# Conditioning and position-bias rows spread over 36 groups, and the first phase and the mixing listed anew by a planner that counts eight places for transfers

## The chip, the core and the metric

One core of a Trainium2 chip runs the whole kernel in one launch. The metric is device time in microseconds (us). The program keeps five queues going: TensorE (PE, with its weight loads PEld), VectorE (DVE), ScalarE (ACT), GpSimd (POOL, nearly unused here) and SyncE (SP), which issues every transfer (DMA). Each queue is worked off in its own fixed order; semaphores tie them together.

## What is computed

One residual block over 512 tokens of width 1024, one layer. Cut to what matters:

```python
mod = silu(c) @ w_ada + b_ada                       # 9 x 1024 numbers: shift, scale, gate of three sites
h = rmsnorm(x, g_ffn1) * (1 + sc1) + sh1
x = x + 0.5 * gt1 * swiglu(h, w_ffn1_in, w_ffn1_down)            # 1024 -> 2 x 2816 -> 1024
h = rmsnorm(x, g_mix) * (1 + sc2) + sh2
q_a, k_a, v_a, q_idx, k_idx, w_idx, c_q, c_kv, k_rope, gates = split(h @ w_in)
score = sum_h w_idx * relu(q_idx . k_idx)           # 8 index heads; the best 128 keys are kept
o_a = softmax(q_a . k_a / 8 + rel_bias[t5_bucket(pos_k - pos_q)], kept keys) @ v_a   # 8 heads, one k, one v
o_b = latent attention from c_q, c_kv, k_rope, causal by blocks of 64                # 8 heads
y = sigmoid(g_a) * (o_a @ w_o_a) + sigmoid(g_b) * (o_b @ w_o_b)
x = x + gt2 * (y @ w_out)
h = rmsnorm(x, g_ffn2) * (1 + sc3) + sh3
x = x + 0.5 * gt3 * swiglu(h, w_ffn2_in, w_ffn2_down)
out = rmsnorm(x, g_final)
```

Two side jobs feed this. **Conditioning** (`ada`): the product `silu(c) @ w_ada` is done as 72 reductions on DVE, each over one 512 KB block of `w_ada`; its result is one column of `mod`. **Position bias** (`t5_rows`): 32 blocks of rows of the bias are made with comparisons on DVE and ACT, 12 small matmuls, a copy on ACT and a transfer to memory; the sparse attention reads them back later.

## The kernel before

Activations lie with the channels on the 128 partitions and the 512 tokens along the free dimension. Every product is made of three float32r matmuls (high and low parts of weights and activations: `mm3`), each weight tile is split on ACT (`wh_...`, a cast) and DVE (`wl_...`, a subtraction).

The stages follow one another. First phase: inputs arrive, the first RMSNorm, and the first group of the first feed-forward layer (`first_group`, line 797: six PSUM banks of products that run through eight input blocks k; for each k the steps `w{k}` weights, `a{8+k}` and `a{k}` conditioning, `g{k}` gain, `m{k}..` modulated input, `f{k}..` products). Then the rest of the first feed-forward layer (`swiglu`, line 1018), the residual and norm at its end (`residual`, line 761: the last three output blocks are done in two halves of the tokens, the norm follows half by half), the mixing (line 1126: first group `hw`, `hm`, `hf`; then index scores `I`, top-k `T`, latents `L`, gates `G`, the two attentions `D`, `E`, `S`, `W`, the output projections `Y`, `O`), and the second feed-forward layer.

**Who sets the order.** While the program is built, `Plan.order` (line 473) plays the kernel through with a duration for each instruction. At each step it takes, on the engine that can start first, the instruction with the lowest place in a list among those that could start within `ahead` ns of the earliest; one that is on the list of urgent steps goes first if it could start within `share` of the other's cost. The order in which it starts them is the order of each engine's queue. Two stretches have lists of their own, `FIRST_ORDER` (line 48) and `MIX_ORDER` (line 87), with a cap for each kind of buffer (`FIRST_CAPS`, `MIX_CAPS`: how many of a kind may be held at once; `ix` are the PSUM banks of the index products, `ada` the blocks of `w_ada`). Elsewhere the program's own order holds. Buffers of one kind are handed out in the list's order of the instructions that fill them (`slot_time`, line 584). A transfer starts, in the plan, when the SP queue is free and its buffer is.

**The two side jobs in the first feed-forward layer.** `fill` (line 1644) is called 43 times, n = 1 to 43: after each of 19 pairs of hidden tiles and with each of 24 output tiles (eight in each of three groups of hidden tiles; the last eight are n = 36 to 43). Each call puts conditioning blocks into the program up to 56 n / `ADA_N`, and bias rows up to 10 + 22 n / `T5_N`:

```python
with nc.after(nc.last_pe):                      # the transfers wait for the matmuls so far
    while todo and 56 - len(todo) < max(min(2 * n, 8), 56 * n / ADA_N):
        self.ada(todo.pop(0))
...
while rows and 32 - len(rows) < T5_0 + (32 - T5_0) * n / T5_N:
    self.t5_rows(rows.pop(0))
```

A product's first matmul in a bank carries `start`, and every other one of that bank depends on it, so the products of k = 0 come first whatever the list says.

Of the kernel before, what the change touches and what calls it, by code (L numbers as in the profile page):

```python
# [19 lines left out]
I32 = mybir.dt.int32  # L20
# [25 lines left out]
URGENT = 2  # L46

FIRST_ORDER = """
t x10 g5 c d1 a0 x02 f10 f50 d5 m01 x03 m10 m00 w1 a11 x11 d4 m20 w0 x12 d0 a8 m11 a10 p n0 x13 f20 m21 g3 w2 m50
f40 f21 r6 f70 a9 g0 d6 r9 g2 a2 d2 m30 v r7 a1 n1 r2 r8 a3 x01 x00 a13 r5 f00 m40 f11 r3 a12 r4 g6 z f30 g4 a5  # L50
w6 m60 a4 r0 g7 w3 f60 r1 w4 m70 a6 d7 w5 w7 f01 a14 a15 d3 a7 g1
"""
FIRST_CAPS, FIRST_AHEAD, FIRST_SHARE = {"ada": 3, "adap": 128, "mt0": 41, "mt256": 110, "nrm": 90, "sg": 48, "t5m": 31, "t5o": 6, "whi": 68, "wlo": 59, "wst": 3}, 80.0, 0.10
FIRST_URGENT = """
c p x00 x01 v w2 n0 n1 f30 g7 m01 m40 f11 r9 f01 a7 a15 g1 m11 d0 m60 z g5 f50 a3 f00 d2 f40 m70 d7 g3 g0 w7 r7
f10
"""
# [25 lines left out]
"""  # L83

MIX_AT = 40
MIX_CAPS, MIX_AHEAD, MIX_SHARE = {"ava": 42, "avb": 20, "gate": 14, "gl": 2, "ix": 4, "lat": 14, "mg": 22, "mm": 60, "mt0": 1, "mt256": 27, "nrm": 32, "os": 7, "osa": 7, "yy": 3, "bias": 3, "mask": 7, "qa": 15, "wst": 1, "pA": 32, "pB": 18, "pTA": 25, "pTB": 36, "pe": 7, "rl": 46, "rn": 30, "score": 38, "t5": 16, "tpa": 24, "uhi": 26, "ust": 1, "wlo": 39, "y": 90}, 60.0, 0.30
MIX_ORDER = """
Yo0 B00 I30 hm00 B02 va Dx00 hf30 D01 hf60 S02 I36 hw1 hm01 hw0 hw5 hf10 S01 I31 u4 W00 L7 Lx4 hw2 Yg1 hf50 Wo1
L6 hm10 B10 W02 S03 I14 pq7 I21 qi1 i11 hw3 hw4 u0 B01 Yg4 I37 Yg3 S00 Ln4 I10 Wo2 L5 L4 hw6 W01 Wo0 Lx6 W12 S10
I35 A3 W10 Wo3 hm20 Yo6 hf20 hw7 L8 E000 i6 B11 I22 Uw I13 D00 ka B03 A1 S13 I26 pq5 pk6 S11 B13 I15 W11 pq2 kr  # L90
W20 W21 I17 I12 Wo5 i7 I16 A2 k1 Sn1 I11 T7 T13 B12 I20 I24 D10 G7 U2 W22 Yg2 pq4 U0 E101 B21 hf41 S12 G2 E201 R0
D02 G9 Lx5 pk2 B20 U3 Eo00 pk3 Yg0 W30 I23 i3 Lx7 i4 xs S23 hf31 i5 Pq0 pq3 S20 B22 k0 W31 i17 Eo10 G0 I32 pq0
Pk0 B31 hm70 E100 I34 B23 Pq1 I27 hm21 I33 hm50 Ln7 pq6 D03 S21 i2 G8 pk1 hf01 Dx10 U1 I25 i1 S22 Pk1 i0 W32 W40
R1 Pk2 i8 i15 hf61 W62 i16 W41 G1 pk5 Sn0 W50 G5 S30 W51 S33 S32 D11 hm41 hm60 T9 Yo1 i9 B30 S31 A0 S42 B32 Wo4
G4 S50 T6 hf71 Pq2 S41 D20 hz i18 W52 G6 B04 E202 u1 hf70 W42 qi3 S53 S40 Sn3 Yo2 G11 B16 T8 Yg7 hm30 E300 S51
qi2 qi0 D31 i10 hf21 ki D12 S52 i14 i12 S43 B33 T15 i20 D13 B14 W60 S60 Eo11 i13 u5 D23 D22 B07 i22 B17 i21 hf11
T10 i19 Wo6 E301 i24 Ya1 S62 Sn2 B06 G12 Yo5 E110 D30 k2 D21 B05 G3 Yb1 hm11 hm40 hm71 D32 i23 S61 D33 D04 S63
Lx8 Yb6 D07 Dx20 Ya0 Yb3 Yg5 Ya5 O2 D14 Ya7 B15 D17 E303 D06 Eo30 Yb0 B25 E302 Yb7 E200 D16 Ya6 D25 W61 Yo3 B37
E111 Ya4 B27 Yb2 hm61 E212 G13 Ya2 Wo7 B24 T12 hf40 T5 E210 hf51 Eo20 B35 O0 D37 Dx01 E312 D05 Sn7 W70 G10 Eo21
O4 Eo31 D27 D15 Sn6 Ya3 S72 O50 pq1 S70 O70 G15 k3 Yb5 Yb4 Yg6 E311 T4 O1 Dx11 Sn5 hf00 E313 B26 D26 u2 Ow5 W72  # L100
S71 hm31 O3 B34 T11 G14 O60 E010 Dx21 Yo4 O71 Pq3 On0 Dx30 E211 O61 D34 pk7 Dx31 D35 u3 D24 hm51 W71 Pk3 O51 pk0
E310 D36 T14 Ow7 Yo7 Sn4 Eo01 On1 pk4 B36 Ow6 S73
# [3 lines left out]
I34 I35 I36 u4 R0 k0 Pk0 pk0 pq1 i16 i11 S02 Sn0 W01 W02 S11 S12 pq2 pq3 W10 W12 Wo1 i18 Sn2 W21 B03 Dx00 Eo00
Sn3 i13 G6 W30 Wo3 Pk2 pq4 pk4 pq5 S40 S41 S42 D10 D11 D13 W42 Wo4 E100 T15 u3 Pq3 k3 Pk3 pk7 T11 D21 B22 S61 S62
S63 Sn6 W50 W51 W52 i12 D30 D31 D32 Dx30 D04 B05 D05 B06 G13 E201 Eo20 B14 D14 B16 D17 Dx11 D24 D25 Dx21 E302
E303 Eo30 E010 E111 i24 B34 D34 D35 B36 Dx31 E210 E211 E212 Eo21 S70 S71 S72 S73 E310 E312 E313 i19 W71 Yg0 Ya1
Yb1 Yb4 Ya5 Yb5 Ya6 On0 i0 G9 Dx01 B26 hf51 D01 I20 B27 hf01 I13 i21 D33 pk6 W62 B33 A1 D26 Ya4 Ow6 B13 hm01 hf61  # L110
# [231 lines left out]
class Plan:  # L342
# [130 lines left out]
    def order(self):  # L473
# [21 lines left out]
        self.free = {c: [(0.0, i) for i in range(n)] for c, n in SLOTS.items()}  # L495
        self.free[BANK] = [(0.0, i) for i in range(N_BANKS)]
        bw, clock, table, began, port = 0.0, Clock(), 1, 0.0, {"dve": 0.0, "pool": 0.0}
        for op in self.ops:
            if not op.left:
                ready[op.eng].append(op)  # L500
        done = []
        while len(done) < len(self.ops):
            best = None
            for e, lst in ready.items():
                if not lst:
                    continue
# [24 lines left out]
                best = (lo, r, op)
# [4 lines left out]
            _, s, op = best  # L536
            e = op.eng
# [6 lines left out]
            if e == "dma":  # L544
                x = max(s + op.hold + 625, bw)
                bw = x + op.cost
                op.end = bw
                free[e] = max(s + op.hold, bw - 3500)
            elif e == "pe":
                op.end = free[e] = s + op.cost * clock.factor(s)  # L550
                clock.busy(s, op.end, op.active)
                began = s
            else:
                op.end = free[e] = s + op.cost
                table = op.table or table
                if op.port:
                    port[e] = op.end
# [1138 lines left out]
```

## Time and profile before

| | us |
|---|---|
| median of three runs (1161.88, 1162.05, 1167.06) | 1162.05 |
| the profiled execution's own time | 1167.69 |
| its span, first to last instruction | 1165.7 |
| PE busy in the span | 1134.9 (97%) |
| DVE busy | 846.5 (73%) |
| ACT busy | 550.3 (47%) |
| mean granted TensorE clock, share of 2.4 GHz | 0.990 |

All durations below come from the profiled execution. In a row of a stretch, the number in brackets is the count of instructions, PEclk the granted clock as a share of 2.4 GHz (0.50 is 1.2 GHz), and the last two columns say how busy the transfer engines were and what they moved. In a row of the timeline the columns are start, length (of the merged instructions), engine, line, operation, output and inputs with their shapes; in brackets the engine's idle time just before it and what ended it. Every instruction of the plan has line 619, the call in `issue`, so one goes by the names of tiles.

### The profile page before, as it was taken

How to read it: one execution, taken by the hardware profiler on the slowest of the kernel's cores; microseconds unless marked ns; L12 is line 12 of the kernel's file. 1: busy time of each engine (PE TensorE's matmuls, PEld its weight loads, DVE VectorE, ACT ScalarE, POOL GpSimd, SP SyncE). 2: the span in 40 equal slices, each digit the busy share in tenths (PEclk: the TensorE clock that was granted, in tenths of full speed). 3: DMA queues.
4: the chain of work that ended last, by engine and by line, in shares of the span. 5: the costliest groups of instructions: out<-in, count | busy, mean ns of one | idle time of the engine just before them, and what ended most of it. 6: DMA issues, size and time to landing. Idle time of an engine off the chain costs nothing. (4 is left out here: it accounts for less than half of the span.)

```text
span 1165.7 us, 17532 instructions
## 1 busy us (share of the span) xinstructions
PE 1134.9 (97%) x6668; PEld 973.2 (83%) x6673; DVE 846.5 (73%) x1650; ACT 550.3 (47%) x1019; POOL 1.0 (0%) x7
## 2 busy tenths in 40 slices
PE   7999999999999999999999998999999999999996
PEld 5888888877887888887787776889999999999986
DVE  6975674558655785579999897757987877777746
ACT  5443333343333255545756678433564444445433
POOL 0000000000000000000000000000000000000000
PEclk9999999999999999999999999999999999999998
DMA  8645566557555743213233347431432333332122
GB/s 305 240 163 198 172 219 201 167 191 268 160 171 176 251 148 110 75 59 98 67 122 101 115 143 244 136 106 57 155 107 84 109 118 91 100 116 86 58 68 73
DMA packets 69590, 164.00 MB, mean 141 GB/s; under 512 B 10321, under 2 KB 22097, under 8 KB 69506
## 3 DMA queue, kind: packets, MB, share of 16 engines
q1 hardware_dynamic: 69506, 162.88, 43.5%
q8 instruction: 52, 0.85, 0.3%
q14 instruction: 32, 0.26, 0.1%
HBM read 148.11 MB, written 13.63 MB: 139 GB/s over the span
## 5 line engine op out<-in xcount | busy, mean ns | idle before, releaser
L619 DVE CUSTOM_DVE_ANT_0 junk<-ada,sc,vecs 128x1024 bf16<-128x1024 f32 x72 | 92.1, 1281 | 31.5 <-DMA ada<-in_w_ada_dram 31.4
L619 PE MATMUL bank<-hmh,wh_ib 128*128 128x512 f32 x200 | 80.5, 404 | 3.5 <-ACT wh_ib L619 2.5
L619 DVE SCALAR_TENSOR_TENSOR x<-bank,gt,x 128x512 f32<-128x512 f32 (+1 forms) x82 | 55.9, 682 | 34.2 <-PE bank L619 34.2
L619 PE MATMUL bank<-hml,wh_ib 128*128 128x512 f32 x200 | 80.5, 402 | 0.0
L619 PE MATMUL bank<-hmh,wl_ib 128*128 128x512 f32 x200 | 80.1, 401 | 0.1
L619 PE MATMUL bank<-hh,wh_1d 128*128 128x512 f32 (+1 forms) x197 | 74.0, 376 | 0.0
L619 PE MATMUL bank<-hl,wh_1d 128*128 128x512 f32 (+1 forms) x197 | 73.6, 374 | 0.0
L619 PE MATMUL bank<-hh,wl_1d 128*128 128x512 f32 (+1 forms) x197 | 73.6, 374 | 0.0
L619 PE MATMUL bank<-hl,wh_2d 128*128 128x512 f32 (+1 forms) x196 | 72.6, 371 | 0.0
L619 PE MATMUL bank<-hh,wh_2d 128*128 128x512 f32 (+1 forms) x196 | 72.4, 370 | 0.0
L619 PE MATMUL bank<-hh,wl_2d 128*128 128x512 f32 (+1 forms) x196 | 72.1, 368 | 0.0
L619 PE MATMUL bank<-f1h,wh_1g 128*128 128x512 f32 x152 | 59.5, 392 | 0.0
L619 PE MATMUL bank<-f1l,wh_1g 128*128 128x512 f32 x152 | 59.2, 389 | 0.0
L619 PE MATMUL bank<-f1h,wl_1g 128*128 128x512 f32 x152 | 59.2, 389 | 0.0
L619 PE MATMUL bank<-f1h,wh_1u 128*128 128x512 f32 x152 | 59.2, 389 | 0.0
L619 PE MATMUL bank<-f1l,wh_1u 128*128 128x512 f32 x152 | 59.2, 389 | 0.0
L619 PE MATMUL bank<-f1h,wl_1u 128*128 128x512 f32 x152 | 59.2, 389 | 0.0
L619 DVE TENSOR_TENSOR wl_1d<-ws_1d,wh_1d 128x896 fp32r<-128x896 f32 (+1 forms) x24 | 27.3, 1136 | 31.9 <-ACT wh_1d L619 21.2
L619 ACT CAST wh_1d<-ws_1d 128x896 fp32r<-128x896 f32 (+1 forms) x24 | 23.5, 979 | 54.5 <-DMA ws_1d<-in_w1d_dram 42.2
L619 PEld LDWEIGHTS bank<-hmh,wh_ib 128*128 128x128 f32 x200 | 38.1, 191 | 12.0 <-ACT wh_ib L619 2.8
L619 DVE TENSOR_TENSOR wl_1u<-ws_1u,wh_1u 128x1024 fp32r<-128x1024 f32 x19 | 23.2, 1223 | 33.5 <-ACT wh_1u L619 33.4
L619 PEld LDWEIGHTS bank<-hh,wh_1d 128*128 128x128 f32 x197 | 38.4, 195 | 7.9 <-issue 1.9
(2076 smaller groups left out, 3459.7 us busy)
## 6 DMA issues: line engine op xcount, KB each, us to landing
ada<-in_w_ada_dram SPq DMA_DIRECT2D x72, 512.0 KB, 4.5
ws_ib<-in_wib_dram SPq DMA_DIRECT2D x25, 512.0 KB, 3.6
ws_1g<-in_w1b_dram SPq DMA_DIRECT2D x19, 512.0 KB, 4.2
ws_1u<-in_w1b_dram SPq DMA_DIRECT2D x19, 512.0 KB, 3.7
ws_f<-in_w2b_dram SPq DMA_DIRECT2D x19, 512.0 KB, 3.7
ws_f<-in_w2b_dram SPq DMA_DIRECT2D x38, 256.0 KB, 3.6
ws_1d<-in_w1d_dram SPq DMA_DIRECT2D x16, 448.0 KB, 3.2
ws_2d<-in_w2d_dram SPq DMA_DIRECT2D x24, 256.0 KB, 2.7
```

The lines of the kernel that those rows point to most:

```text
L619: op.fn(*[real(v) for v in op.args], **{k: real(v) for k, v in op.kw.items()})
```

## The change

`T5_N` goes from 40 to 36 and `ADA_N` from 41 to 36. The lists, caps, `ahead`, `share` and urgent steps of the first phase and of the mixing are replaced. In `order`, a transfer may start no earlier than 1000 ns after the end of the eighth-last transfer; that rule holds in all stages, while the orders of the two feed-forward layers after the first group are not listed.

```diff
 FIRST_ORDER = """
-t x10 g5 c d1 a0 x02 f10 f50 d5 m01 x03 m10 m00 w1 a11 x11 d4 m20 w0 x12 d0 a8 m11 a10 p n0 x13 f20 m21 g3 w2 m50
-f40 f21 r6 f70 a9 g0 d6 r9 g2 a2 d2 m30 v r7 a1 n1 r2 r8 a3 x01 x00 a13 r5 f00 m40 f11 r3 a12 r4 g6 z f30 g4 a5
-w6 m60 a4 r0 g7 w3 f60 r1 w4 m70 a6 d7 w5 w7 f01 a14 a15 d3 a7 g1
+d5 a1 t n0 p d7 x10 d0 m00 x01 f20 x03 m01 v f10 g3 w2 g0 d6 m10 d1 g2 m20 f30 f60 a8 x02 a9 r3 n1 a11 g1 g7 m11
+d2 r8 a0 g6 w0 g5 d3 a2 x11 f50 g4 c f01 x12 m21 w1 m30 w3 f21 a7 x13 r6 z m40 f70 a10 x00 f11 r5 r1 r0 f40 r4 a3
+m50 m60 w4 a12 a13 a4 w5 a5 w6 r2 a14 d4 r9 r7 a15 m70 a6 w7 f00
 """
-FIRST_CAPS, FIRST_AHEAD, FIRST_SHARE = {"ada": 3, "adap": 128, "mt0": 41, "mt256": 110, "nrm": 90, "sg": 48, "t5m": 31, "t5o": 6, "whi": 68, "wlo": 59, "wst": 3}, 80.0, 0.10
+FIRST_CAPS, FIRST_AHEAD, FIRST_SHARE = {"ada": 23, "adap": 146, "mt0": 58, "mt256": 145, "nrm": 117, "sg": 63, "t5m": 38, "t5o": 13, "whi": 78, "wlo": 73, "wst": 2}, 60.0, 0.00
 FIRST_URGENT = """
-c p x00 x01 v w2 n0 n1 f30 g7 m01 m40 f11 r9 f01 a7 a15 g1 m11 d0 m60 z g5 f50 a3 f00 d2 f40 m70 d7 g3 g0 w7 r7
-f10
+c p x00 x01 v n1 x03 w2 x02 r6 m60 x11 r7 x12 a6 a1 m50 m01 m30 m11 g4 a12 a15 x13 f10 d4 r3 r5 a11 d1 w7 d2 g2
+g0 f11 a4 w6 r2 a0 a2 m00 f50 g1
 """
-T5_0, T5_N, ADA_N = 10, 40, 41
+T5_0, T5_N, ADA_N = 10, 36, 36
...
-MIX_CAPS, MIX_AHEAD, MIX_SHARE = {"ava": 42, "avb": 20, "gate": 14, "gl": 2, "ix": 4, "lat": 14, "mg": 22, "mm": 60, "mt0": 1, "mt256": 27, "nrm": 32, "os": 7, "osa": 7, "yy": 3, "bias": 3, "mask": 7, "qa": 15, "wst": 1, "pA": 32, "pB": 18, "pTA": 25, "pTB": 36, "pe": 7, "rl": 46, "rn": 30, "score": 38, "t5": 16, "tpa": 24, "uhi": 26, "ust": 1, "wlo": 39, "y": 90}, 60.0, 0.30
+MIX_CAPS, MIX_AHEAD, MIX_SHARE = {"ava": 31, "avb": 20, "gate": 15, "gl": 3, "ix": 1, "lat": 4, "mg": 15, "mm": 49, "mt0": 7, "mt256": 26, "nrm": 33, "os": 2, "osa": 13, "yy": 5, "bias": 3, "mask": 3, "qa": 19, "wst": 1, "pA": 33, "pB": 17, "pTA": 32, "pTB": 31, "pe": 10, "rl": 53, "rn": 17, "score": 22, "t5": 15, "tpa": 19, "uhi": 20, "ust": 1, "wlo": 38, "y": 67}, 20.0, 0.30
 MIX_ORDER = """
...
 MIX_URGENT = """
...
+        self.lanes = [0.0] * 8
...
-                    r = max(op.ready, t + 1500.0 * (op.table not in (0, table)), began + op.load if e == "pe" else 0.0)
+                    r = max(op.ready, self.lanes[-8] + 1000.0 if e == "dma" else 0.0, t + 1500.0 * (op.table not in (0, table)), began + op.load if e == "pe" else 0.0)
...
                 bw = x + op.cost
                 op.end = bw
+
+                self.lanes.append(bw)
```

`MIX_ORDER` and `MIX_URGENT` are whole new lists of the same steps (some 560 in the order).

## Rows read from the trace of the kernel before

**Rows 1.** Busy time by stretch, whole kernel but the tail.

```profile
0.00:30.00 30.00, 22.27 (x214) 16.05 (x217) 20.41 (x82) 17.27 (x47) 0.70 (x6) 0.94 0.90 307
30.00:68.00 38.00, 37.85 (x227) 32.02 (x228) 36.44 (x77) 19.18 (x34) 0.00 (x0) 0.96 0.65 230
60.00:403.00 343.00, 343.00 (x1729) 280.45 (x1728) 211.04 (x306) 120.00 (x171) 0.31 (x1) 1.00 0.61 197
403.00:428.00 25.00, 21.26 (x140) 19.84 (x139) 20.89 (x62) 11.24 (x22) 0.00 (x0) 0.86 0.39 126
428.00:525.00 97.00, 96.07 (x532) 82.28 (x530) 61.44 (x105) 51.64 (x86) 0.00 (x0) 1.00 0.28 91
525.00:650.00 125.00, 121.28 (x578) 95.72 (x577) 121.36 (x321) 78.79 (x183) 0.00 (x0) 0.99 0.29 92
650.00:735.00 85.00, 80.03 (x422) 62.64 (x424) 69.57 (x194) 65.59 (x161) 0.00 (x0) 1.00 0.55 179
735.00:1150.00 415.00, 415.00 (x2832) 385.38 (x2831) 302.75 (x493) 189.94 (x322) 0.00 (x0) 1.00 0.31 96
```

**Rows 2.** Busy time by stretch: the three places where the clock falls.

```profile
29.00:34.00 5.00, 5.00 (x33) 4.28 (x33) 4.61 (x13) 1.36 (x4) 0.00 (x0) 0.57 0.99 357
405.00:413.00 8.00, 7.79 (x40) 7.77 (x40) 4.59 (x19) 2.19 (x5) 0.00 (x0) 0.57 0.41 126
526.00:532.00 6.00, 4.11 (x11) 3.26 (x12) 5.82 (x11) 3.93 (x7) 0.00 (x0) 0.72 0.28 92
```

**Rows 3.** Timeline of DVE at the end of the first feed-forward layer.

```profile
399.26 0.42 DVE L619 TENSOR_TENSOR acc_n<-acc_n,sq_n 128x256 f32<-128x256 f32 x1
401.92 1.28 DVE L619 CUSTOM_DVE_ANT_0 junk<-ada,sc,vecs 128x1024 bf16<-128x1024 f32 x1 [2.24 <-DMA ada<-in_w_ada_dram]
403.13 0.48 DVE L619 SCALAR_TENSOR_TENSOR x<-bank,gt,x 128x256 f32<-128x256 f32 x1
403.53 1.28 DVE L619 CUSTOM_DVE_ANT_0 junk<-ada,sc,vecs 128x1024 bf16<-128x1024 f32 x1
404.73 0.42 DVE L619 TENSOR_TENSOR acc_n<-acc_n,sq_n 128x256 f32<-128x256 f32 x1
```

**Rows 4.** Timeline of PE there.

```profile
402.90 0.28 PE L619 MATMUL bank<-hh,wl_1d 128*128 128x256 f32 x1
403.02 0.28 PE L619 MATMUL bank<-hh,wh_1d 128*128 128x256 f32 x1
405.20 0.87 PE L619 MATMUL bank<-ones,acc_n 128*128 128x2 f32 x4 [1.91 <-DVE acc_n L619]
406.93 0.41 PE L619 MATMUL bank<-hh,wh_1d 128*128 128x256 f32 x1
407.14 0.41 PE L619 MATMUL bank<-hl,wh_1d 128*128 128x256 f32 x1
```

**Rows 5.** Timeline of SP: the last two conditioning blocks are issued.

```profile
395.25 0.86 SPq L619 DMA_DIRECT2D ada<-in_w_ada_dram  x2
```

**Rows 6.** Busy time by stretch: output tiles of the first group of hidden tiles.

```profile
125.00:175.00 50.00, 50.00 (x302) 40.52 (x301) 33.99 (x54) 18.47 (x31) 0.31 (x1) 1.00 0.63 203
```

**Rows 7.** Timeline of the first phase: ACT, DVE and PE.

```profile
4.82 1.06 ACT L619 ACTIVATE sc<-c 128x1024 f32<-128x1024 f32 x1 [2.40 <-DMA c<-in_c_dram]
11.98 4.98 PE L619 MATMUL bank<-x 128*128 128x128 f32 x24 [1.36 <-DMA x<-in_xT_dram]
24.31 4.97 PE L619 MATMUL bank<-ones,sq_n 128*128 128x2 f32 x32
27.10 1.27 DVE L619 SCALAR_TENSOR_TENSOR mf1h<-x,a,bank 128x256 f32<-128x256 f32 x3
29.81 0.58 PE L619 MATMUL bank<-f1h,wh_f 128*128 128x256 f32 x1
```

**Rows 8.** Timeline of PE in the mixing.

```profile
527.89 0.50 PE L619 MATMUL bank<-hmh,wh_ib 128*128 128x512 f32 x1 [2.03 <-ACT wh_ib L619]
```

**Rows 9.** What SP waited for from 505 to 530 us: total, times, longest.

```profile
SPq L619 <- DVE wl_uk L619: 9.7, 1, 9.7
SPq L619 <- ACT gl L619: 8.2, 1, 8.2
```

**Rows 10.** The tile `rl`, ACT's reading of the index products: ns, first and last start.

```profile
L619 ACT ACTIVATE rl<-bank x24: 380/492/606, 468.2 to 526.1; 128x512 f32<-128x512 f32 x8, 128x256 f32<-128x256 f32 x8, 128x384 f32<-128x384 f32 x8
```

More of the change, by code (lines that the diff above doesn't have):

```diff
@@ L87 @@
 MIX_ORDER = """
[L88 to L102, printed above, removed]
+hf31 hf70 u0 S00 hw0 hm30 hw4 Wo0 Yg6 S01 S02 u4 S03 hw1 I10 Lx6 Dx00 I14 qi0 I31 pq7 pq6 I30 pk6 hm00 hw2 W00
@@ new lines @@
+B00 I13 B02 Yg4 B11 D01 E100 I21 pq5 S10 hw5 L7 Yo6 I37 B01 Yg1 hm20 i1 W02 Uw hf41 Lx4 hw3 I22 i17 I36 D02 L6 L5
+I16 L4 A3 W01 E000 I12 u1 B03 k0 Wo1 W12 B10 hm10 qi1 i7 D00 S13 hw7 W10 S11 hw6 va W11 hf20 hm21 Lx5 A1 kr I15
+I26 W21 i20 ka L8 A2 I17 I11 I20 B21 U1 B13 W22 S12 Ln4 Yo4 E101 G7 G2 Wo3 U0 I24 Sn1 W20 I35 pk3 W30 pq2 B12 T15
+R0 Lx7 G9 U2 i6 D10 I23 pq0 Pq0 S23 pq3 U3 B20 i0 i9 i5 B22 i4 I32 W31 I25 Dx10 hm50 D20 Pk0 S20 I27 B31 i3 S21
+pk5 hf71 i8 Ln7 hm01 Yg5 Pq1 E201 W32 Pk1 pk1 I33 W40 i2 D03 B23 B30 S22 Eo00 hf00 I34 G0 G8 B32 pk4 Yg2 k1 R1 G5
@@ new lines @@
+pk2 W62 G1 S32 W50 S30 S33 hm61 S31 T10 W41 T8 B04 S42 B14 D11 S50 E202 hf21 W51 B33 Yo1 i16 Sn3 hm71 u5 B16 i11
+Pk2 S41 G4 D31 A0 Lx8 W42 O70 E301 i18 S40 S51 i10 W52 Pq2 i14 Sn2 S52 T7 S43 Yo0 S53 i13 T13 i15 i12 D12 S60 G6
+Yg0 i19 Wo4 D13 G3 hf51 B07 G12 ki i22 Sn4 i21 S61 i24 S73 T5 D23 E110 Yg3 E200 Ya1 D30 D22 Yo3 xs Sn0 B17 G11
+E300 D21 Wo5 T4 D32 Yb1 Wo6 Eo10 Wo7 Pq3 hf30 D33 k2 Yo5 i23 S63 B05 D04 Yb6 hm41 qi3 D07 B06 pq4 Yb7 W61 D14 T9
+Ya5 E303 Wo2 E302 D17 hf11 E212 D06 O50 G13 Eo20 W60 hm31 B25 hf60 Ya0 qi2 S62 Dx20 D25 B37 pq1 Ya4 pk7 G10 Eo11
@@ L103 @@
+T12 Yb5 Ow7 B15 Ya2 O1 hf50 Eo30 D37 T6 Ya7 Yb3 Eo01 Yb0 E111 Yo2 Eo21 D05 D15 Dx11 Ya3 W70 D16 O2 E210 Ya6 S72
+D27 E211 Dx21 E311 B24 G15 D26 Yb4 hm11 S70 Pk3 Ow6 hf61 hz W71 k3 Yb2 Ow5 hf10 Dx01 O3 T11 u2 hm60 S71 Eo31 D24
+Dx31 O0 Yg7 B27 B34 T14 hf40 O60 Sn7 O4 E010 B26 E313 O51 hf01 Yo7 Sn5 D35 O71 hm40 On0 E310 O61 B36 E312 D34
+hm70 Dx30 pk0 hm51 D36 G14 On1 W72 u3 Sn6 B35
 """
 MIX_URGENT = """
-hz hm00 hm11 hf11 hm20 hm21 hf50 hf60 xs qi1 qi3 kr i1 I10 I15 I16 I17 Ln4 i7 L7 Lx7 Lx8 I22 I23 I24 I25 I26 I32
@@ L106 @@
[L106 to L110, printed above, removed]
@@ L111 @@
-hf71 I12 hm70 hf41 pq7 B23 B00 i2 qi0 Eo10 i3 B07 hm10 hf21 i15 Uw D22 W11 pk3 hw7 D15 D06 L5 B31 D02 Ow5 i4 hm30
-Ow7 B11 D23 hf20 hf31 Yo7 B02 E301 hw2
+hm11 hm30 hm31 hm40 ki qi0 I15 I16 Ln4 Lx7 Lx8 I22 I23 I24 I26 I35 R0 k0 pk0 i11 Sn0 S11 S12 pq2 pk2 pq3 W10 Wo1
+i18 Sn2 B00 Dx00 Sn3 i13 G6 W30 Pk2 pk4 pq5 S40 S41 B11 D11 Wo4 E100 u3 Pq3 k3 Pk3 pk7 D21 S61 S62 S63 Wo5 i12
+D31 i22 G13 E201 Eo20 D16 Dx11 B25 Dx21 E303 Eo30 E010 E111 D34 D35 Dx31 E210 E211 E212 S70 S71 S73 E310 E311
+E312 E313 i19 W71 Yo0 Yb4 Ya6 O1 On0 Dx01 I12 S51 hm51 Eo00 Lx5 pk6 Yo4 i2 I21 Ya2 E101 D25 E110 W01 E301 pk5 I31
@@ L113 @@
+D20 B20 B27 B30 T7 D07 B23 i14 hm01 hm71 O4 S23 hf30 D12 Ow5 W00 D06 Eo21 B15 Yo1 D14 B35 hf21 D17 Yo5 B06 i16
+hw7 W41 qi2 U0 D02 hm70 D10 W11 L5 Yo2 hf51 O70 Yg2 E202 A1 i7 S33 hw3 hf50 hf01 D22 i15 hf70 hw2 Ow6 pq7 hf10
+E200 B21 S31 S00 W20 u0 i8 i5 I34 W72 Yg6 xs Yg3 D24 hf60 Yg4 D30 hm10 Yb0 B04 i9 S72 D05 Wo6 W52 D04 u1 hm20 Sn5
+hf71 I30 D37
 """
```

## The prediction

> **What bounds the kernel now.** I read the busy time by stretch first. From 60 to 403 us and from 735 to 1150 us PE has no idle time at all and the full clock [rows 1]: there the end is set by the matmuls alone, the change takes none away and adds none, and no order of other queues can make these 758 us shorter. What can change lies in three places. In the first 30 us PE is busy for 22.27, so 7.7 us are idle; from 30 to 68 us it is busy for 37.85 of 38, while DVE is busy for 36.44, so DVE keeps up only just [rows 1]. From 403 to 428 us, where the first feed-forward layer hands over to the mixing, 3.7 us of PE are idle. In the mixing 0.9 us are idle up to 525, 3.7 from 525 to 650 and 5.0 from 650 to 735; in the middle one of these DVE is busy for 121.36 of 125 us, so it is DVE that paces it, and in the stretch before, DVE still has 35.6 us free [rows 1].
>
> The second view is the granted clock. Three spells are at 1.2 GHz instead of 2.4. A mean of 0.57 over 5 us is 5 x 0.43 / 0.5 = 4.3 us at half speed, which costs 2.1 us; 0.57 over 8 us is 6.9 us, a cost of 3.4; 0.72 over 6 us is 3.4 us, a cost of 1.7 [rows 2]. The second and the third follow an idle PE: 1.91 us before 405.20 and 2.03 before 527.89 [rows 4, 8].
>
> Last, the timelines around these places say who was late.
>
> **How the execution stands to the median.** The profiled execution took 1167.69 us (span 1165.7, so 2.0 around it), the runs 1161.88, 1162.05 and 1167.06. The median is 5.6 us below the execution in which I read my rows. The spells of slow clock cost 7.2 us together in that execution, and I cannot see whether the shorter runs have them all. I therefore count idle time in full and the cost of a slow spell by half when I go down from the median, and in full when I go down from 1167.69.
>
> **The conditioning and the bias rows.** Before, the 56 conditioning blocks were complete only at n = 41, the first half of the third-last output tile. SP issues the last two at 395.25 [rows 5], and DVE, which works in order, sits idle for 2.24 us until one lands at 401.92, reduces it in 1.28 us, does one residual add at 403.13, reduces the other from 403.53 and only then adds the squares for the norm at 404.73 [rows 3]. PE is at its last matmul at 403.02, and waits 1.91 us for exactly that sum [rows 4]. Behind the two reductions on DVE stand the residual add, the sum of squares and so the norm, and behind the norm the whole mixing; ACT's squares wait for the residual add.
>
> With 36 both jobs are complete at n = 36, the first of the last eight output tiles, four full tiles and a half earlier. A full tile is 7 blocks of 3 matmuls of 512 columns; at two half tiles of 0.12 us a matmul [rows 4] that is 21 x 0.24 = 5.0 us, so the last block is asked for about 22 us earlier, near 373. Without the two reductions the sum of squares would be there 2 x 1.28 = 2.56 us earlier even if nothing is credited for the wait for the transfer: at 405.15 - 2.56 = 402.6, before PE asks at 403.3. So the stall of 1.91 us goes, and with it very likely the slow spell behind it: matmuls of 256 columns follow each other every 0.21 us there instead of 0.12 [rows 4]. Next late is the norm's own chain, which PE has to cover with the two half tiles that are left, 42 x 0.12 = 5.0 us; I allow 0.5 us for that. This is worth 1.91 + 3.4 - 0.5 = 4.8 us in the profiled execution and 1.91 + 1.7 - 0.5 = **3.1 us** from the median; the bounds are 0 (another late step on DVE takes their place) and 5.3.
>
> The work itself is moved, not removed. Per call it becomes 56/36 - 56/41 = 0.19 more blocks, 0.24 us of DVE and 0.1 MB, and 0.06 more bias rows. Beside output tiles of 5 us DVE has 16 of 50 us free and the transfer engines are busy at 0.63 [rows 6]; over the whole stretch DVE is busy for 211 of 343 us [rows 1]. I cost this at nothing. Without that cover it would be 0.24 us a call, 8.6 us over 36 calls. SP issues the same transfers, five or six calls earlier, and past them the first weights of the mixing move up.
>
> **The first phase.** PE begins the feed-forward products at 29.81 [rows 7]. Ahead of them in its queue stand 4.97 us of squares sums from 24.31, and DVE makes the first modulated input only at 27.10. How early can they begin with the new lists? Buffers are handed out in list order, so the conditioning blocks come as 1, 8, 9, 11, 0; k = 0 needs blocks 8 and 0, and its products must be first. Before block 0 has landed, some 5.8 MB must have: x with 2.1, c with 0.5, five blocks with 2.6, one tile of weights and the constants with 0.6. At the 307 GB/s of the first 30 us [rows 1] that is 18.9 us, so about 20 us; a reduction of 1.28, one modulation of 0.4 and the cast bring 23 to 24, an estimate. The gain at the start is thus at most 5.8 us. On the other side c, the first transfer before, now comes behind a block, the constants and a weight tile, some 1.1 MB or 3.6 us: `silu(c)`, begun at 4.82 [rows 7], begins near 8.4, and every conditioning reduction waits for it. If DVE loses that much it is a loss of 3.6 us, since DVE paces the 38 us that follow. Between a gain of 5.8 and a loss of 3.6 I take **2.5 us of gain**: nearer to the gain, as the 24 products of x that the norm needs end at 17 [rows 7], and the 12 us from there to the first product are queueing on DVE and PE more than data that had not come; but less than half of it, because DVE has to do the same work in the stretch up to 68.
>
> **The mixing's list and the eight places.** The one large stall is that before 527.89: 2.03 us of PE and the 1.7 us of slow clock behind it, for a weight tile that came late [rows 2, 8]. SP's waits just before were for a DVE subtraction (9.7 us) and an ACT copy (8.2 us), not for an earlier transfer [rows 9], so the rule of eight places doesn't remove it by itself; a list that places these steps anew may or may not. The bounds: all idle time from 428 to 735 and this spell, 9.6 + 1.7 = 11.3 us of gain; a loss of 11.8 us (the second rival). I take half of the one stall, (2.03 + 0.85) / 2 = **1.4 us of gain** (1.9 in the profiled execution), as DVE, at 97% from 525 to 650, leaves an order little room [rows 1]. In the second feed-forward layer the rule only moves transfers in SP's queue; PE has no idle time there, and I cost it at nothing; if a weight tile came late there, one such stall is the 3.7 us of 527.89.
>
> **Sum.** From the median: 1162.05 - 3.1 - 2.5 - 1.4 = **1155.0**. A profiled execution like that before: 1167.69 - 4.8 - 2.5 - 1.9 = 1158.5.
>
> **The rivals.**
>
> 1. The lists bring nothing and only the handover gains: 1162.05 - 3.1 = 1159. For it speaks that DVE paces both listed stretches and its work stays; against it, that PE waits in both for order and not for DVE's throughput alone [rows 7, 8]. A like time, 1158, comes out if the change doesn't do what it says, the last blocks still landing late because SP's queue holds them back, while the lists gain their 3.9.
>
> 2. Slower: the index products lose their banks. The cap `ix` falls from four PSUM banks to one. There are 24 such products, and ACT reads each in 0.492 us [rows 10]. If PE must wait for each reading before the next product, that is 24 x 0.492 = 11.8 us, 1155.0 + 11.8 = 1166.8, and one more fall of the clock of the 2.6 us between the two in the mixing and the handover [rows 2] makes it 1169.4. It decides from 0.29 us a product (7.0 / 24), where the gain is eaten. Against it: PE has the large products of the input projection to put between, and up to 525 it is idle for 0.9 us only [rows 1]. The Trainium skill, Perfetto Trace Analysis, section Matmuls, speaks for this rival: independent groups of matmuls should rotate through PSUM banks, so that the reading of one overlaps the next. No run here shows one bank; by that rule the time would be that of this rival, by the row of 0.9 us idle the forecast's.
>
> 3. Everything is gained: 5.8 in the first phase, the full 4.8 at the handover, half of the 11.3 in the mixing: 1162.05 - 16.2 = 1146. It needs DVE to run ahead before 525.
>
> **How the numbers follow.** The forecast holds 0.50 of the chance (1152 to 1158.5, three fifths of it below 1156.2), the first rival with its variant 0.20, the second 0.11, the third 0.19. About 0.5%, 5.8 us, is what a measurement of this kernel can tell from no change. Faster by more than that (below 1156.2): 0.30 + 0.19 = 0.49; within: 0.20 + 0.20 = 0.40; slower: 0.11. The range goes from 1147 to 1167; it leaves out the slow rival and the lower half of the third.
>
> **What would show it.** Right: no conditioning reduction on DVE after about 385 us, no PE wait for `acc_n` at the end of the first feed-forward layer and full clock there; the first feed-forward product before 27 us and the first one after the first group before 67; no PE wait over 1 us for `wh_ib`. Wrong: a new wait of PE in place of that for `acc_n`, a feed-forward start later than 30 us with DVE waiting for `sc`, PE waiting for `rl` again and again between 460 and 530, or PE idle time after 735.

## The result and the profile after

The changed kernel takes 1154.44 us (median; 1153.21 to 1155.74), the kernel before beside it 1162.05 us; the ratio is 0.9924 with a 95% interval from 0.9902 to 0.9945. The forecast was 1155.0. Its sum came out near by luck: two of its three terms have the wrong size and nearly make up for each other, as the experiments show.

Busy time by stretch of the changed kernel, in the columns of [rows 1]; the stages now end up to 13 us earlier, so the later stretches begin a little further on in the work:

```profile
0.00:30.00 30.00, 23.41 (x225) 16.80 (x226) 21.48 (x85) 17.51 (x49) 0.70 (x6) 0.91 0.95 313
30.00:68.00 38.00, 38.00 (x232) 32.67 (x232) 36.30 (x71) 18.49 (x29) 0.00 (x0) 0.98 0.64 226
60.00:403.00 343.00, 340.98 (x1701) 277.10 (x1701) 214.27 (x316) 122.50 (x178) 0.31 (x1) 1.00 0.61 196
403.00:428.00 25.00, 23.67 (x191) 22.95 (x190) 22.57 (x65) 12.83 (x25) 0.00 (x0) 1.00 0.47 142
428.00:525.00 97.00, 94.51 (x501) 80.02 (x500) 68.97 (x140) 48.39 (x80) 0.00 (x0) 0.98 0.30 93
525.00:650.00 125.00, 124.00 (x616) 98.78 (x616) 118.58 (x308) 85.85 (x201) 0.00 (x0) 1.00 0.30 97
650.00:735.00 85.00, 84.80 (x439) 68.78 (x438) 69.95 (x173) 61.38 (x148) 0.00 (x0) 1.00 0.57 188
```

From 525 to 735 us PE's idle time falls from 8.7 us [rows 1] to 1.2. From 403 to 428 us PE does 2.4 us more, at full clock. From 428 to 525 us DVE does 69.0 us of work where it did 61.4 [rows 1]. And there are 2.0 us of idle time in the first feed-forward layer, which had none. Waits of PE over the whole changed kernel (in all, times, longest, us):

```profile
PE bank L622 <- DVE dg_n L622: 4.3, 3, 2.5
PE bank L622 <- DVE posf L622: 2.5, 1, 2.5
PE bank L622 <- ACT t5m L622: 1.8, 1, 1.8
...
PE bank L622 <- ACT kil L622: 1.1, 1, 1.1
PE bank L622 <- ACT wh_ib L622: 0.7, 1, 0.7
```

The waits for `acc_n` [rows 4] and the 2.03 us for `wh_ib` [rows 8] are gone. The 1.8 us for `t5m`, a mask of the bias rows, stand at 257 us and are new there; the kernel before waits 0.8 us for one, at 21 us.

The stages of all runs, by the starts of products in PE's timeline: the first product after the first group, the last one of the first feed-forward layer, the first one of the second. "Mixing" is from the second to the third; the second feed-forward layer takes 350.1 to 350.3 us in the four profiles of the two kernels.

| kernel | first group ends | layer 1 | mixing |
|---|---|---|---|
| before | 68.1 | 346.1 | 389.6 |
| before, again | 69.4 | 341.6 | 389.5 |
| changed | 65.1 | 345.1 | 380.2 |
| changed, again | 66.5 | 342.8 | 378.9 |
| `ADA_N` 41 | 66.4 | 344.2 | 382.2 |
| both numbers back | 67.3 | 341.5 | 382.8 |
| no rule of eight | 67.2 | 343.2 | 380.8 |
| old first list | 67.0 | 341.2 | 380.0 |
| old mixing list | 66.5 | 342.6 | 388.2 |
| top-k late | 66.4 | 343.4 | 388.6 |
| DVE work at 530 to 580 | 66.5 | 343.0 | 385.0 |
| DVE work at 448 to 456 | 66.6 | 342.0 | 388.6 |
| DVE work at 514 to 530 | 66.0 | 342.4 | 388.1 |
| weights first | 66.8 | 376.3 | 380.6 |

The kernels below ran in three groups, each on a chip of its own beside the kernel before, so they are compared by their ratio to it. For the changed kernel that is 0.9924 and, run again, 0.9909; I use 0.9917. A thousandth is 1.16 us, and each ratio is uncertain by 1.2 to 2.6 thousandths either way.

### The profile page after: what moved, and what is told of

Same layout as the page of the kernel before. It is cut to its first block, busy times and chain, and to the rows that moved or that the text cites. A ratio compares the mean times of both kernels' runs of the same rounds, so it can differ in the third digit from the quotient of the medians.

```text
span 1152.7 us, 17526 instructions
## 1 busy us (share of the span) xinstructions
PE 1129.1 (98%) x6673; PEld 969.7 (84%) x6673; DVE 847.2 (73%) x1650; ACT 548.0 (48%) x1019; POOL 1.0 (0%) x7
## 4 chain that ended last, share of the span: by engine, by line
PE 90%; DVE 6%; DMA 2%; ACT 1%; issue 1%; SPq 0%; DVEq 0%; ACTq 0%
PE bank L622 90%; DVE score L622 1%; DMA ws_1d<-in_w1d_dram 1%; DMA x<-in_xT_dram 1%; DVE tiny_top L622 1%; DVE tiny_norm L622 1%; DVE tiny_mla L622 0%; DMA ws_ib<-in_wib_dram 0%; DVE mhmh L622 0%; DVE junk L622 0%; DVE qa L622 0%; DVE wl_ib L622 0%; DVE o L622 0%; DVE hml L622 0%; ACT qa L622 0%
```

## One part undone at a time

**The numbers of 36.**

```diff
-T5_0, T5_N, ADA_N = 10, 36, 36
+T5_0, T5_N, ADA_N = 10, 36, 41
```

> The changed kernel with ADA_N back at 41, so that the last conditioning blocks come at n = 41 again; T5_N stays at 36. Theory (the handover gains by the earlier blocks): DVE reduces two blocks after 395 us again, PE waits 1 to 2 us for acc_n at the end of the first feed-forward layer, with slow clock behind it, and the time is 1154.4 + 3.1 = 1157.5 (up to 1159.2 with all of the slow spell). If the new stall at 257 us (1.8 us idle and about 1.7 us of slow clock) comes from the denser conditioning blocks, it is gone here and gives 3.5 back: 1154 to 1156, and PE has no wait for t5m near 257. Rival (the earlier blocks bring nothing, the handover is free for another reason): no wait for acc_n, 1154.4.

1156.25 us, ratio 0.9929 (0.9908 to 0.9950): 1.4 us above the changed kernel. PE waits 1.6 us for `acc_n` and 1.6 for `hmh`, the first modulated input of the mixing; there is no idle time at 257 us. With both numbers back (`10, 40, 41`):

> The changed kernel with T5_N = 40 and ADA_N = 41 as before; lists, caps and the rule of eight places stay. Theory (the earlier conditioning is worth the handover's stall, less what the denser blocks cost near 257 us): a PE wait of 1 to 2 us for acc_n near 405 us and slow clock after it, no PE idle time from 250 to 262 us, time 1 to 3 us above the changed kernel, 1154 to 1157. Rival (the forecast's term in full, nothing lost elsewhere): 3.1 us above it or more, 1156 to 1158.5. Second rival (the handover is covered by the new lists anyway): 1153 to 1154, no wait for acc_n.

1155.13 us, 0.9922 (0.9906 to 0.9937): 0.6 us above. There is again no idle time at 257 us, and PE waits twice at the handover:

```profile
403.87 0.61 PE L622 MATMUL bank<-ones,acc_n 128*128 128x2 f32 x4 [1.09 <-DVE acc_n L622]
412.51 0.96 PE L622 MATMUL bank<-hmh,wh_hm 128*128 128x256 f32 x6 [1.64 <-ACT hmh L622]
```

From 396 to 420 us PE is idle for 4.1 us with `ADA_N` at 41 and 3.5 with both numbers back, with a spell of slow clock in each; with 36 it is idle for 1.0, at full clock. In the table the mixing is about 2 us longer with 41. So at the handover itself the numbers of 36 gain 2.5 to 3.1 us of idle time and the slow spells, which is what was forecast or more. But they trade one stall for another, the one at 257 us, and what is left in the time, 0.6 to 1.4 us, is less than these ratios can tell from nothing.

**The rule of eight places.**

```diff
-                    r = max(op.ready, self.lanes[-8] + 1000.0 if e == "dma" else 0.0, t + 1500.0 * (op.table not in (0, table)), began + op.load if e == "pe" else 0.0)
+                    r = max(op.ready, t + 1500.0 * (op.table not in (0, table)), began + op.load if e == "pe" else 0.0)
```

> The changed kernel without the rule of eight places for transfers in the plan; lists, caps and the two numbers of 36 stay. Theory (the lists make the gain, the rule only moves transfers): first product of the second feed-forward layer within 3 us of 790.4, time 1152 to 1158. Rival (the rule is what takes the waits out of the mixing): the mixing, from the first hm product to the first product of the second feed-forward layer, gets back most of the 11 us that it lost, 385 to 390 us instead of 378, and the time is 1161 to 1165. If the stall at 257 us comes from the rule, PE has no wait over 1 us there.

1154.21 us, 0.9913 (0.9891 to 0.9935): no difference. The mixing takes 380.8 us, and the idle time near 257 us stays. The rule is not the gain.

**The first phase's list**, with its caps, `ahead`, `share` and urgent steps, is that of before:

```diff
 FIRST_ORDER = """
-d5 a1 t n0 p d7 x10 d0 m00 x01 f20 x03 m01 v f10 g3 w2 g0 d6 m10 d1 g2 m20 f30 f60 a8 x02 a9 r3 n1 a11 g1 g7 m11
+t x10 g5 c d1 a0 x02 f10 f50 d5 m01 x03 m10 m00 w1 a11 x11 d4 m20 w0 x12 d0 a8 m11 a10 p n0 x13 f20 m21 g3 w2 m50
...
```

> The changed kernel with the first phase's list, caps, ahead, share and urgent steps of the kernel before. Theory (the new list gains 2.5 to 3.0 us by the end of the first group): first feed-forward product near 29.8 us instead of 28.5, last product of the first group near 68 instead of 65, time 1154.4 + 2.5 to 3.0 = 1157 to 1157.4. Rival (the gain of the start is given back later, or came from the rule of eight places): end of the first group at 65 us, 1154.4.

1154.05 us, 0.9915 (0.9891 to 0.9939): no difference, which is the rival's time. The first group ends at 67.0 us, 0.6 later than the average of the new list, but the rest of the first layer takes 341.2 us, where the kernels with the new list and `ADA_N` at 36 take 342.0 to 345.1 (the last row of the table apart): the idle time at 257 us is gone with the new list.

**The mixing's list**, from `MIX_CAPS` to `MIX_URGENT`, is that of before:

```diff
 MIX_ORDER = """
-hf31 hf70 u0 S00 hw0 hm30 hw4 Wo0 Yg6 S01 S02 u4 S03 hw1 I10 Lx6 Dx00 I14 qi0 I31 pq7 pq6 I30 pk6 hm00 hw2 W00
+Yo0 B00 I30 hm00 B02 va Dx00 hf30 D01 hf60 S02 I36 hw1 hm01 hw0 hw5 hf10 S01 I31 u4 W00 L7 Lx4 hw2 Yg1 hf50 Wo1
...
```

> The changed kernel with the mixing's list, caps, ahead, share and urgent steps of the kernel before. By the forecast's term the new list is worth 1.4 us: 1155.8. By the two traces it is worth about 11 us in the mixing: first hm product to first product of the second feed-forward layer near 389 us instead of 378, time near 1165; by the two medians, less what the other parts were forecast at, about 2 to 4: 1156.5 to 1158.5. Rival (the old list is good with the rule of eight places): 1154.4.

1161.50 us, 0.9981 (0.9966 to 0.9996): 7.5 us above the changed kernel, and 388.2 us of mixing. PE waits 2.0 us for `wh_ib` again, here up to 521 us, and is idle for 1.2 and 4.7 us in the next two stretches:

```profile
525.00:650.00 125.00, 123.80 (x600) 97.25 (x599) 120.63 (x334) 80.80 (x189) 0.00 (x0) 1.00 0.31 98
650.00:735.00 85.00, 80.30 (x413) 63.09 (x416) 69.23 (x178) 62.44 (x151) 0.00 (x0) 1.00 0.55 176
```

That is nearly all of the gain.

## What in the mixing's list

In the two kernels I compared what DVE does on either side of 525 us. A round of the top-k is one MAX8 and one MATCH_REPLACE8. Groups of DVE instructions with these steps; first before from 455 to 525 and from 525 to 650 us, then the changed kernel in the same two stretches (count, busy us, mean ns, idle time before):

```profile
L619 DVE MAX8 tiny_top<-score 128x8 f32<-128x256 f32 x2 | 0.8, 422 | 0.0
L619 DVE MATCH_REPLACE8 score<-tiny_top,score 128x256 f32<-128x256 f32 x1 | 0.4, 406 | 0.0
L619 DVE MATCH_REPLACE8 score<-tiny_top,score 128x384 f32<-128x384 f32 (+2 forms) x45 | 24.7, 551 | 0.0
L619 DVE MAX8 tiny_top<-score 128x8 f32<-128x384 f32 (+2 forms) x44 | 24.4, 562 | 0.2
```

```profile
L622 DVE MAX8 tiny_top<-score 128x8 f32<-128x256 f32 x16 | 6.8, 426 | 0.4
L622 DVE MATCH_REPLACE8 score<-tiny_top,score 128x256 f32<-128x256 f32 x16 | 6.5, 409 | 0.0
L622 DVE MATCH_REPLACE8 score<-tiny_top,score 128x384 f32<-128x384 f32 (+1 forms) x32 | 19.3, 606 | 0.0
L622 DVE MAX8 tiny_top<-score 128x8 f32<-128x384 f32 (+1 forms) x32 | 19.1, 611 | 0.0
```

The 16 rounds of the second token block (the forms with 256 keys) are done before 525 us now; 49.1 - 38.4 = 10.7 us of top-k have left the stretch from 525 to 650 us, in which DVE is busy for 97% before. Four runs test whether this is the reason. The changed kernel again is the measure beside them:

> The changed kernel once more, unchanged but for a comment, as the measure for the three runs beside it and to see what differs from one execution to the next. Theory (the end of the first group and the stall at 257 us vary with the arrival of transfers, not with the queues' order): the first group ends between 65.1 and 67.2 us, PE's idle time from 250 to 262 us is between 0 and 2 us. Rival (both belong to the order): 65.1 us again and 1.8 us again. Time 1153 to 1156.

1152.94 us, 0.9909 (0.9884 to 0.9935). The end of the first group is 66.5, and the idle time from 250 to 262 us is 1.27.

**Top-k late.** In the finished order, 12 of those rounds are held back on DVE:

```diff
+        for op in self.order():
+            if op.eng == "dve" and op.step in ("T5", "T6", "T7") and op.fn.__name__ in ("max", "match_replace"):
+                held.append(op)
+                continue
+            done.append(op)
+            n += op.eng == "dve" and op.start > 512000.0
+            if op.eng == "dve" and op.start > 512000.0 and held and n % 6 == 0:
+                done += held[:2]
+                del held[:2]
```

> The changed kernel with 12 of the 16 top-k rounds of the second token block (T5, T6, T7: MAX8, MATCH_REPLACE and the load of the found values, 12 x (0.426 + 0.409 + 0.090) = 11.1 us of DVE) issued later on DVE: out of 465 to 485 us, one round after every sixth DVE instruction from about 527 us on. Nothing else moves in any queue. Theory (the new mixing list gains because it does top-k work before 525 us, where DVE has time, and takes it out of the stretch that DVE paces): the mixing gets longer by 7 to 11 us, time 1161 to 1165, DVE busy for over 120 of 125 us from 525 to 650. Rival (the gain lies in PE's own order and in the weight tiles; the mask that these rounds feed is made only near 620 us, so they may be late): within 2 us of the changed kernel.

1161.23 us, 0.9981 (0.9965 to 0.9996): 8.3 us above the changed kernel beside it, within the theory's 7 to 11. Its row of the middle stretch and PE's waits there:

```profile
525.00:650.00 125.00, 117.52 (x565) 92.43 (x563) 119.74 (x322) 78.42 (x182) 0.00 (x0) 0.99 0.29 88
```

```profile
PE bank L633 <- DVE pBl L633: 2.5, 4, 0.9
PE bank L633 <- DVE kl L633: 2.0, 2, 1.8
PE bank L633 <- ACT pB L633: 0.9, 1, 0.9
PE bank L633 <- DVE qa L633: 0.9, 1, 0.9
```

PE is idle for 7.5 us of 125, where the changed kernel is for 1.0, and it waits for DVE's splits (`pBl`, `kl`, `qa`). DVE's 119.7 us missed the 120 that I had asked for; the length of the mixing bears the theory out. So the new list needs this work out of the middle stretch: with it back, all that the list had gained is lost.

The loss does not come back in the old list's places, though. There PE stands for `wh_ib` (2.0 us, with slow clock behind it) and from 650 to 735 us (5.0 us [rows 1]); with top-k late it waits 0.6 us for `wh_ib` and is idle for 0.2 us from 650 to 735. The waits from 650 on of the kernel before, and that stretch with top-k late:

```profile
PE bank L619 <- DVE pA L619: 1.3, 2, 0.8
PE bank L619 <- ACT pAh L619: 1.3, 1, 1.3
```

```profile
650.00:735.00 85.00, 84.81 (x450) 68.29 (x450) 69.61 (x180) 65.50 (x162) 0.00 (x0) 1.00 0.54 179
```

That the early rounds are also what took the old list's stalls away is thus an inference: no run has the old list with these rounds early.

**DVE work put in.** The changed kernel with 20 needless MAX8 (0.40 to 0.41 us each), in three places:

```diff
+            n += op.eng == "dve" and op.start > 512000.0
+            if op.eng == "dve" and op.start > 512000.0 and n <= 100 and n % 5 == 0:
+                dve.max(out=scr, in_=vecs)
```

> The changed kernel with 20 needless MAX8 instructions on DVE (some 0.42 us each, 8.4 us in all), one after every fifth DVE instruction from about 527 us on; the output is not touched. Theory (DVE paces 525 to 650 us): 5 to 8.4 us longer, 1159.5 to 1163. Rival (PE's order and the transfers pace it, DVE's 95% are no bound): under 2 us, 1154 to 1156.

1158.12 us, 0.9950 (0.9930 to 0.9969): 5.2 us more for 8 us of work. DVE's time in the middle costs about two thirds of itself, within the theory's range.

In one piece, earlier:

```diff
+            if op.eng == "dve" and op.start > 424000.0 and n < 20:
+                for n in range(1, 21):
+                    dve.max(out=scr, in_=vecs)
```

> The changed kernel with the same 20 needless MAX8 instructions on DVE (8.4 us in all) in one piece after the subtraction of the last hm weight tile, near 436 us, where DVE is busy for 13 of 30 us. Theory (DVE has time there): 0 to 2 us longer, 1154 to 1156.5. Rival (any DVE work in the mixing costs its own time): 8 us, 1162.

1160.76 us, 0.9975 (0.9961 to 0.9989): 7.8 us more. Here the rival was right. The piece stood at 447.7 to 456.2 us, later than I had put it, and behind it in DVE's queue was the cast of the index key:

```profile
460.45 0.58 PE L625 MATMUL bank<-kih,qi 128*128 128x256 f32 x1 [6.92 <-DVE kih L625]
```

And two at a time, between those places:

```diff
+            if op.eng == "dve" and op.start > 499000.0 and n < 20:
+                for n in range(n + 1, n + 3):
+                    dve.max(out=scr, in_=vecs)
```

> The changed kernel with the 20 needless MAX8 on DVE (8.2 us in all), two after each of ten DVE instructions between about 513 and 530 us, where DVE is busy for 8.5 of 15 us. Theory (time that DVE has free can be filled where no product waits for the next DVE instruction): 0 to 2 us longer, 1153 to 1156. Rival (DVE has no time to give anywhere in the mixing, as the piece of 8.3 us ahead of the key's cast cost 7.8 us): 6 to 8 us longer, 1159 to 1161.

1161.53 us, 0.9979 (0.9967 to 0.9990): some 7 us above the changed kernel; the rival again, though DVE has 6.5 of these 15 us free. Behind the added work stands the chain of small steps of a norm, and PE waits for its end, with the clock at 0.77 after it:

```profile
533.90 2.07 PE L625 MATMUL bank<-dg_ckv,ones 128*128 128x512 f32 x2 [5.32 <-DVE dg_ckv L625]
```

```profile
530.00:545.00 15.00, 11.10 (x39) 8.38 (x40) 12.42 (x31) 4.40 (x12) 0.00 (x0) 0.77 0.16 53
```

So my picture of DVE was half right. Its time from 525 us on is scarce, and the new list depends on having top-k out of it. But "DVE has time before 525" is not what makes that free: the changed kernel's DVE is idle for 10.3 of the 15 us from 440 to 455 and for 6.5 of those from 515 to 530, and 8 us more cost 7 to 8 at either place. Nearly free is the place near 465 to 485 us, where the rounds now stand. The stretch from 470 to 485 us in the kernel before, the changed one, and the one with top-k late:

```profile
470.00:485.00 15.00, 15.00 (x75) 12.69 (x74) 5.35 (x7) 9.03 (x19) 0.00 (x0) 1.00 0.26 75
```

```profile
470.00:485.00 15.00, 15.00 (x68) 12.45 (x68) 13.93 (x37) 6.71 (x12) 0.00 (x0) 1.00 0.30 101
```

```profile
470.00:485.00 15.00, 15.00 (x69) 12.44 (x68) 11.70 (x27) 6.31 (x11) 0.00 (x0) 1.00 0.27 97
```

PE is busy all the time in each, though DVE is busy for 13.93 of 15 us in the changed one. Over the whole stretch before 525 us the rounds cost PE little: it is idle for 2.5 us with them and for 2.0 with 12 of them held back.

```profile
428.00:525.00 97.00, 94.98 (x506) 81.44 (x505) 61.13 (x109) 49.55 (x81) 0.00 (x0) 0.98 0.30 95
```

I take it that nothing that PE needs soon is queued behind the rounds; no run puts other work there.

## The stalls that come and go

> The kernel before once more, unchanged but for a comment, to see which of the stalls read in its first profile belong to every execution. Theory (the handover's stall and the one before 527 us are in the order, the start varies with the transfers): PE waits 1.5 to 2.5 us for acc_n and about 2 us for wh_ib again; the end of the first group moves by up to 2 us from 68.1; time 1160 to 1167. Rival (the 5.6 us by which the first profile lay above the median are one of these two stalls): one of them is missing, and the span is 5 us shorter by that alone.

1164.62 us, 1.0008 (0.9992 to 1.0023). The stall of the mixing is there again (`wh_ib`, 1.9 us), and the mixing takes 389.5 us. The stall of the handover is not:

```profile
401.74 1.28 DVE L619 CUSTOM_DVE_ANT_0 junk<-ada,sc,vecs 128x1024 bf16<-128x1024 f32 x1 [1.13 <-DMA ada<-in_w_ada_dram]
405.03 0.61 PE L619 MATMUL bank<-ones,acc_n 128*128 128x2 f32 x4 [0.34 <-DVE acc_n L619]
```

The queues are those of [rows 3, 4], but the block is 1.1 us less late relative to DVE (1.13 against 2.24), so PE waits 0.34 us in place of 1.91, and the clock stays at 1.00 from 396 to 420 us. The 346.1 - 341.6 = 4.5 us of layer 1 between the two profiles are this one stall with its slow clock. The rival of the expectation had the mechanism: as far as two executions can tell, most of the 5.6 us by which the first profile lay above the median were one stall that an execution may have or not. (The span is only 2.8 us shorter, as the first group ends 1.3 us later here.)

The new stall at 257 us is of the same kind. SP's queue in the changed kernel there, and the two engines that wait in a row (ACT for the weight tile, PE for the mask that ACT makes behind it):

```profile
244.16 5.14 SPq L622 DMA_DIRECT2D ada<-in_w_ada_dram  x3
249.39 1.79 SPq L622 DMA_DIRECT2D ws_1d<-in_w1d_dram  x1
251.28 2.78 SPq L622 DMA_DIRECT2D ada<-in_w_ada_dram  x2
254.34 0.33 SPq L622 DMA_DIRECT2D ws_1d<-in_w1d_dram  x1
```

```profile
256.30 0.94 ACT L622 CAST wh_1d<-ws_1d 128x896 fp32r<-128x896 f32 x1 [10.23 <-DMA ws_1d<-in_w1d_dram]
```

```profile
258.23 0.35 PE L622 MATMUL bank<-t5m,t5w 128*32 128x448 bf16 x1 [1.82 <-ACT t5m L622]
```

Issues of conditioning blocks stand ahead of the tile. SP waits there for matmuls and buffers: from 225 to 262 us 14.0 us for PE's banks and 4.6 for DVE's `mod`, which I put down to these blocks, and 4.7 for `wl_1d`. Eight profiles with `ADA_N` = 36 and the new first list have 0.5 to 2.0 us of idle time there (mean 1.3); those with 41, and the one with the old first list, have none. I tried to mend it: in SP's queue of this layer each block's issue goes behind the next weight tile's, unless its reduction on DVE would come first:

```diff
+            if op.eng == "dma" and op.start > 68000.0 and any(b.tag == "ada" for b in op.allocs):
+                nxt = [j for j in range(i + 1, min(len(done), i + 400)) if done[j].eng == "dma" and done[j].start < op.start + 5000.0
+                       and any(b.tag in ("wst", "w1st") or b.name.startswith("ws_1") for b in done[j].allocs)]
+                use = min(at[id(u)] for u in op.users)
+                if nxt and nxt[0] < use:
+                    key[i] = nxt[0] + 0.5
```

> The changed kernel with one rule more on SP's queue in the first feed-forward layer: the issue of a conditioning block is put behind the next issue of a weight tile, where its reader on DVE stands later than that. Nothing else moves. Theory (the idle time near 257 us is a weight tile whose issue stands behind conditioning blocks that wait for their buffer): PE has no wait for t5m and under 0.3 us idle from 250 to 262 us, the handover stays free, and the time is 1 to 3 us lower, 1150.5 to 1153. Rival (the wait is for the bias rows' masks on ACT, whatever SP issues): the wait stays, same time as the changed kernel, 1153 to 1154.5.

1187.79 us, 1.0203 (1.0183 to 1.0222): 33 us slower than the changed kernel, and neither expectation was near. The reductions kept their places in DVE's queue, ahead of the instructions that make `wl_1d` and `hl`, and now most find their block still on the way. What DVE waited for from 60 to 430 us, in this kernel and in the changed one run again:

```profile
DVE junk L632 <- DMA ada<-in_w_ada_dram: 90.5, 33, 5.6
```

```profile
DVE junk L622 <- DMA ada<-in_w_ada_dram: 27.0, 25, 3.2
```

The early issue of the blocks was the cover of their flight. The run shows that the 1.3 us at 257 are not to be had by this move of SP's issues alone; I expect that the reductions on DVE would have to move with them, and that was not tried.

## The prediction, step by step

**Mixing, -1.4 us: wrong by its size.** The list is worth 7.5 us (old list back). The step that failed is "I take half of the one stall", with its reason, "as DVE, at 97% from 525 to 650, leaves an order little room". It took DVE's work in that stretch as given. The list moves 10.7 us of it across the stretch's border; put back, 12 of these rounds cost 8.3 us. And the reason speaks of 525 to 650 us only: the 5.0 us of PE's idle time from 650 to 735 [rows 1], more than the one stall, stand in the bounds but not in the term. Of the 8.7 us idle behind 525, 1.2 are left. The third rival named the condition, "It needs DVE to run ahead before 525", and gave half of the bound for it.

**Handover, -3.1 us: mechanism right, size wrong.** The last reductions come at 375.63 and 380.13 us, PE has no wait for `acc_n`, and the clock is full from 400 to 420 us, as forecast. But the numbers back cost only 0.6 to 1.4 us in all. Two terms were mis-sized. The stall was read from one execution as if each had it; it is 1.91 and 0.34 us in the two profiles of before and, in the two kernels with 41, 1.6 and 1.1 us (these also wait 1.6 us for `hmh`, which the forecast did not have). And "I cost this at nothing" for the moved work was wrong where SP is the queue in question: the row of the transfer engines (0.63 busy [rows 6]) says nothing on issues that wait ahead of a weight tile, 1.3 us of PE on average. The first norm wait behind the handover was put at 0.5 us; in the changed kernel PE waits 0.69 us for `sq_n` at 411.65.

**First phase, -2.5 us: the start moved by about that, its owner and its worth are open.** In the two profiles of before the first group ends at 68.1 and 69.4 us, in the ten with the new list and the rule at 65.1 to 67.3, 66.4 on average: 2.3 us less. But taking the list alone away costs nothing (0.9915 against 0.9917), nor does taking the rule alone away (0.9913), and with either one the group ends at 67.0 and 67.2 us, once each. Which of the two carries the start can't be told from that; nor does the time show that an earlier start is kept, as without the new list the idle time at 257 us goes too. The first product began at 28.52 us, not at 23 to 24, and not before 27, which was one of the forecast's own signs: its input was there at 24, but PE's queue had 32 matmuls of the squares' sums from 23.02 us on ahead of it. The estimate went by the data and left out PE's queue, which the same paragraph had named.

**Second feed-forward layer, nothing:** right, 350.1 us against 350.3.

**The rivals.** The slower one, PE waiting for the readings of the index products, did not happen: the 24 readings run from 457.4 to 532.1 us, and only DVE ever waited for one (0.5 us). The cap `ix` had been misread: it holds the plan to one index product at a time, not to one bank. In the changed kernel's plan the 24 products pass through all eight banks, and none takes the bank of the one before. The rule of the Trainium skill, Perfetto Trace Analysis, section Matmuls, that independent groups should rotate through PSUM banks, is kept there, so no run here shows what breaking it would cost. (The range up to 1167 did not quite leave this rival out: its lower figure was 1166.8.) The first rival, lists that bring nothing, is refuted by the run with the old mixing list. The third had the mixing's gain nearest, 5.7 us, and too much in the other two places.

That the forecast was near the result is luck: -3.1 that shrank to about -1 and -1.4 that grew to -7.5 nearly made up for each other, against a median of before that was 1162.05 here and 1163.10 to 1164.58 in the other three groups of runs.

## What to carry to other kernels

Where an engine paces a stretch, ask which of its work is due only later and could be done before the stretch; its load there depends on the order. Where such work can go is not told by the busy share: 8 us more of DVE work cost 7 to 8 us in stretches where DVE was idle for 6.5 and 10.3 of 15 us, while the rounds stand, at a cost of about 0.5, in one where it is now 93% busy. Look at what is queued behind the place, and at who waits for it. A stall that hangs on a transfer landing just in time should be read from several executions before it is put into a sum; and an issue moved back in the queue of transfers needs its reader moved with it.

## What the runs showed of the hardware

A like idle time of PE is followed by a slow clock in one execution and not in another, with the same order of queues. Stretches behind the stall at 257 us, in the changed kernel (a wait of 1.82 us, then 3.4 us at half speed) and in the kernel with top-k late (a wait of 1.67 us, no slow clock):

```profile
257.00:259.00 2.00, 0.57 (x2) 0.09 (x1) 1.74 (x3) 2.00 (x6) 0.00 (x0) 1.00 1.02 414
259.00:261.00 2.00, 2.00 (x8) 1.53 (x8) 2.00 (x5) 2.00 (x5) 0.00 (x0) 0.75 0.82 310
261.00:263.00 2.00, 2.00 (x6) 1.61 (x5) 2.00 (x5) 2.00 (x4) 0.00 (x0) 0.50 0.27 99
263.00:265.00 2.00, 2.00 (x9) 1.61 (x9) 1.51 (x3) 1.54 (x3) 0.00 (x0) 0.89 0.72 203
```

```profile
257.00:259.00 2.00, 0.77 (x17) 0.21 (x6) 0.53 (x1) 1.50 (x3) 0.00 (x0) 1.00 1.00 365
259.00:261.00 2.00, 1.37 (x5) 0.75 (x5) 2.00 (x5) 2.00 (x5) 0.00 (x0) 1.00 0.72 277
261.00:263.00 2.00, 2.00 (x10) 1.63 (x10) 2.00 (x4) 2.00 (x5) 0.00 (x0) 1.00 0.77 294
```

Of the eight profiles with idle time at 257 us only the changed kernel's first one has a slow spell there; behind the waits of 1.9 to 2.03 us for `wh_ib` in the two profiles of before and the one with the old mixing list each has one. The forecast's half price for a slow spell is thus neither borne out nor refuted. When a spell comes, its price, here 1.7 us, nearly doubles that of the idle time.
